# Forgetting attention: a head's keys and queries in three transfers of 128 rows, head 0's ahead of a store and the mask

## The chip, the cores and the metric

The kernel runs on one core of a Trainium2 chip, as one launch. The metric is the device time of that core in microseconds, the median over the runs of a kernel. The core has a matmul engine (TensorE, PE in the profile, with its weight loads shown apart as PEld), a vector engine (VectorE, DVE), an engine for activations and copies (ScalarE, ACT), a general one (GpSimd, POOL) and a sync engine (SyncE, SP), which here only issues transfers. Each engine takes its own instructions in order; semaphores tie them together. Transfers between the chip's memory (DRAM) and the core's on-chip memory (SBUF, 128 partitions) are carried out by 16 DMA engines. They are issued from queues: SPq is SP's, ACTq and POOLq are those of ACT and POOL.

## The reference, cut to what matters

One layer of a streaming encoder on 1024 frames of width 1024: a norm, one input projection shared by three token mixers (a gated recurrence, forgetting attention and cross-attention to 256 memory tokens), gates, an output projection, and then a gated convolutional feed-forward part. The change concerns the forgetting attention: 8 heads of width 64 over blocks of 128 queries.

```python
def _fox_mixer(q, k, v, f_logit, f_bias, q_g, k_g):
    ...
    log_f = jax.nn.log_sigmoid(f_logit.astype(jnp.float32) + f_bias.astype(jnp.float32))
    Fc = jnp.cumsum(log_f, axis=1).transpose(0, 2, 1)
    scale = FOX_DH ** -0.5
    outs = []
    for blk in range(T // Q_BLOCK):
        lo, hi = blk * Q_BLOCK, (blk + 1) * Q_BLOCK
        s = (jnp.einsum('bhqd,bhkd->bhqk', qh[:, :, lo:hi], kh[:, :, :hi]) * scale
             + Fc[:, :, lo:hi, None] - Fc[:, :, None, :hi])
        mask = (lo + jnp.arange(Q_BLOCK))[:, None] >= jnp.arange(hi)[None, :]
        p = jax.nn.softmax(jnp.where(mask, s, -jnp.inf), axis=-1)
        outs.append(jnp.einsum('bhqk,bhkd->bhqd', p, vh[:, :, :hi]))
```

## The kernel before, in words

Every float32 matmul is done on a high and a low part of its operands (`split`: ACT casts to the shorter format, DVE subtracts to get the rest), as three products `high*high + high*low + low*high` (`mm3`, lines 122 to 124). Large projections go by a scheme with seven block products instead of eight. The kernel goes through the input projections, the forgetting attention, the recurrence, the merge, the output projection and the feed-forward part.

**Where the keys and queries lie.** `put_fqk` (line 647) norms and turns the keys and queries of a pair `p` of heads and stores them in the DRAM tensor `kqd[p]` of shape 2 x 128 x 2 x 1024 (line 655; the last of these stores is issued at 319.44 us, just before the change's place). Index 0 of the first dimension is the keys, 1 the queries; the 128 rows are two heads of 64; then comes high or low part; then 1024 frames. A row of one part is 4 KB.

**Loads of a head.** `fox_load(h)` (line 1012) fills three tiles of 128 partitions x 1024: `kh` holds the keys' high part in both halves, `qa` the queries' high part above their low part, `kl` the keys' low part in both halves. So one matmul of `qa` with `kh` (line 1046) gives high*high + low*high, and one with `kl` (line 1047) adds the rest. Each tile is filled by two transfers of 64 rows (lines 1016 and 1017). Then come two broadcasts of the cumulated forget logits, `nf` (1020), and the values, `vhl` (1022). `kh`, `qa` and `kl` exist twice, for even and odd heads. A head's loads are queued on SPq behind the previous head's first store of results (`yd<-yp`, line 1093); the tile `yp` has a single buffer.

**Attention of a head.** `fox_attn(h)` (line 1027) goes through the 8 query blocks in pairs: POOL adds the mask `mskf` to a block of `nf` (1040), PE makes the logits (1046, 1047), DVE adds the bias and takes the maximum (1052), ACT takes the exponential (1062), POOL scales by the sum's reciprocal (1064), PE turns the result and multiplies by the values (1075 to 1088), ACT and DVE bring it out (1091, 1092).

**What runs beside it.** The input projections of the recurrence and the gates (`cm_unit`, line 808) come in units. A unit loads four weight blocks `ur` (818), adds some of them up on POOL (`us`, 758), casts them on ACT and DVE (`uh`, `ul`, 752 and 753), and has seven products; the results pass through the tile `uo`, of which there are two (803, 804, 796, 797), to a store on SPq (`put_hg`, line 805) or POOL's queue (798), or for gates on ACT's. The first six of the seven steps of unit 0 are laid out ahead of the attention (line 998). They hold the store of the recurrence's queries of head 0, second half of the frames (line 805), which the change moves.

**What sets the order.** Python code lays out all instructions; a planner then orders those of each engine and queue before the run, by priority and by a timeline that it works out with costs of its own. `weave` mixes attention steps with projection steps; `ahead(..., AHEAD)` and `tc.high_priority(n)` give instructions the priority of a place `n` instructions earlier (`AHEAD` is 300); `tc.issue_after(x)` queues what stands in its block behind `x`, if on the same engine, without a wait for `x` to finish. The mask `mskf` is loaded with a priority of 600 instructions ahead (line 1010), `resets` (1007) with none.

Of the kernel before, what the change touches and what calls it, by code (L numbers as in the profile page):

```python
# [9 lines left out]
F32 = mybir.dt.float32  # L10
# [5 lines left out]
P = 128  # L16
T = 1024
# [16 lines left out]
AHEAD = 300  # L34
# [35 lines left out]
def tile_block(ctx: ExitStack, tc: tile.TileContext, xT, x_rows, memT, vec, fbias, mats, hmask, w_ff, w_tm, w_cm,  # L70
               w_mkv, w_br, w_out, w_up, w_dn, outT):
    nc = tc.nc
    V, S, G, PE, SP = nc.vector, nc.scalar, nc.gpsimd, nc.tensor, nc.sync
# [69 lines left out]
    def combine(dst, ps, e, c):  # L143

        if e is None:
            S.activation(dst, ps, AF.Copy, scale=-1.0 if c else 1.0)
        elif c:
            V.scalar_tensor_tensor(out=dst, in0=ps, scalar=-1.0, in1=e, op0=ALU.mult, op1=ALU.subtract)
        else:
            V.tensor_add(dst, ps, e)  # L150
# [6 lines left out]
    kqd = [tc.dram_tile([2, P, 2, T], F32, name=f"kqd{p}") for p in range(4)]  # L157
# [615 lines left out]
    def out_tile():  # L773
        return ur.tile([P, HB], F32, tag="uo", name="uo", bufs=2)

    def put_gate(i):
# [7 lines left out]
            S.dma_start(gd[i, n], t)  # L784
        return put

    def put_hg(what, h):
        def put(c, n, ps, e):
            t = out_tile()
            dst = hgd[h][what][:, n * HB:(n + 1) * HB]  # L790
            if what == 0:
                if e is None:
                    S.activation(t, ps, AF.Tanh, scale=-0.5)
                else:
                    combine(t, ps, e, c)
                    S.activation(t, t, AF.Tanh, scale=0.5)
                G.tensor_scalar(t, t, TMIN, TMAX, ALU.max, ALU.min)
                G.dma_start(dst, t)
                return
            else:  # L800
                z = e if e is not None else ur.tile([P, HB], F32, tag="ue", name="ue", bufs=3)
                combine(z, ps, e, c)
                S.activation(t, z, AF.Tanh, scale=0.5)
                V.scalar_tensor_tensor(out=t, in0=t, scalar=1.0, in1=z, op0=ALU.add, op1=ALU.mult)
            SP.dma_start(dst, t)
        return put

    def cm_unit(u, puts):
# [43 lines left out]
    def puts_of(what, i):  # L852
        return put_gate(i) if what == "gt" else put_hg("fqg".index(what), i)
# [152 lines left out]
    resets = pf.tile([P, 256], F32, tag="resets", name="resets")  # L1006
    SP.dma_start(resets, mats[:, 3 * P:3 * P + 256])
    mskf = pf.tile([P, P], F32, tag="mskf", name="mskf")
    with tc.high_priority(2 * AHEAD):
        SP.dma_start(mskf, mats[:, 2 * P:3 * P])  # L1010

    def fox_load(h):
        p, a = h // 2, slice(64 * (h % 2), 64 * (h % 2) + 64)
        kh, qa, kl = (pf.tile([P, T], F32R, tag=f"{t}{h % 2}", name=f"{t}_{h}") for t in ("kh", "qa", "kl"))
        for t, (u, v) in ((kh, (0, 0)), (qa, (2, 3)), (kl, (1, 1))):
            SP.dma_start(t[0:64, :].bitcast(F32), kqd[p][u // 2][a, u % 2, :])
            SP.dma_start(t[64:128, :].bitcast(F32), kqd[p][v // 2][a, v % 2, :])
        nf = [pf.tile([P, HB], F32, tag="nf", name="nf", bufs=3) for _ in range(2)]
        for n, t in enumerate(nf):
            SP.dma_start(t, negFd[h:h + 1, n * HB:(n + 1) * HB].partition_broadcast(P))  # L1020
        vhl = pf.tile([P, 8, P], F32R, tag="vhl", name="vhl", bufs=2)
        SP.dma_start(vhl.bitcast(F32), vhd[h // 4][:, :, h % 4, :])
        return kh, kl, qa, vhl, nf
# [3 lines left out]
    def fox_attn(h):  # L1027
        p, a = h // 2, slice(64 * (h % 2), 64 * (h % 2) + 64)
        with tc.issue_after(marks["head"].ins) if h else nullcontext():
            kh, kl, qa, vhl, nf = fox_load(h)  # L1030
# [725 lines left out]
    for a, b, own, first, c, n, sign, last, xq in (  # L1756
# [6 lines left out]
        dst = banks if own else ybanks  # L1763
# [130 lines left out]
```

## Time and profile before

| | |
|---|---|
| median of 3 runs | 1677.19 us (1676.16 to 1678.06) |
| profiled execution, its own time | 1679.46 us |
| its span, first to last instruction | 1677.7 us |
| mean granted clock of PE | 0.998 |
| busy: PE, DVE, ACT, POOL | 1654.1, 1215.9, 845.5, 441.4 us |
| `kh`, `qa`, `kl`: loads, size, median from issue to landing | 16 each, 256 KB; 4.0, 5.0, 6.4 us |
| first and last issue of a `kh` load | 322.3 and 617.2 us |

The profile is that of one execution; a row of a timeline gives start and duration in us, engine, line, operation, output and input tiles, shape and count, and in brackets how long the engine stood idle before and what released it. Rows with SPq, ACTq or POOLq are issues of transfers: their duration is that of the issue, not of the transfer. The view of the transfers counts packets (contiguous pieces moved, and tiny ones that close a transfer) and gives for each group the time from issue to landing.

### The profile page before, as it was taken

The page shows a single profiled execution, that of the slowest core. Times are in us where ns is not written, and L with a number is a line of the kernel's source. Part 1 is how long each engine was busy: PE and PEld are TensorE (multiplying, and loading weights), DVE is VectorE, ACT ScalarE, POOL GpSimd, SP SyncE. Part 2 cuts the span into 40 slices and gives each one's busy share as a digit, 9 for nine tenths or more (in the row PEclk, how much of TensorE's full clock was granted, in tenths as well). Part 3 has the DMA queues.
Part 4 walks back from the last instruction along what each step waited for, and adds up shares of the span by engine and source line. Part 5 has one row for each costly group of instructions (what it writes and reads, how often), then busy time and mean ns, then how long its engine had stood idle before and what let it go on. Part 6 is the DMA issues. An engine that isn't in the chain of part 4 may idle for free.

```text
span 1677.7 us, 24989 instructions
## 1 busy us (share of the span) xinstructions
PE 1654.1 (99%) x8915; PEld 1417.1 (84%) x8915; DVE 1215.9 (72%) x2179; ACT 845.5 (50%) x1453; POOL 441.4 (26%) x469
## 2 busy tenths in 40 slices
PE   8999999999999999999999999999999999999999
PEld 7989999777788888888888888888888888888887
DVE  7875766588786766678776868978878788675664
ACT  8655554466666565556333257544434434343332
POOL 1143543455444444223011052221111111100000
PEclk9999999999999999999999999999999999999999
DMA  7253352655455552646866899666544454394782
GB/s 283 98 189 103 130 180 107 200 191 164 157 164 154 151 157 103 200 133 217 317 183 174 253 215 224 175 190 179 146 132 126 153 149 130 133 390 150 239 283 87
DMA packets 132061, 298.20 MB, mean 178 GB/s; under 512 B 14008, under 2 KB 31672, under 8 KB 131296
## 3 DMA queue, kind: packets, MB, share of 16 engines
q1 hardware_dynamic: 100576, 210.08, 36.9%
q0 software_dynamic: 22144, 71.84, 16.8%
q10 hardware_dynamic: 9216, 14.68, 2.3%
q8 instruction: 70, 1.15, 0.3%
q14 instruction: 55, 0.45, 0.1%
HBM read 216.40 MB, written 103.22 MB: 191 GB/s over the span
## 4 chain that ended last, share of the span: by engine, by line
PE 54%; DMA 1%; DVE 0%; ACT 0%; issue 0%
PE pp L122 10%; PE pp L123 10%; PE pp L124 10%; PE lg L124 4%; PE lg L122 4%; PE lg L123 4%; PE tr L122 3%; PE tr L124 3%; PE tr L123 3%; PE po L124 1%; PE po L122 1%; PE po L123 1%; DMA yd<-hz 1%; PE lg L1194 1%; PE lg L1185 0%; PE po L1227 0%
## 5 line engine op out<-in xcount | busy, mean ns | idle before, releaser
L1374 ACT CAST wh<-s 128x512 fp32r<-128x512 f32 x84 | 51.5, 620 | 119.1 <-PE pp L123 62.5
L128 ACT CAST dwh<-wr 128x1024 fp32r<-128x1024 f32 (+1 forms) x41 | 40.2, 980 | 114.9 <-PE tr L123 39.2
L1527 POOL DMA_DIRECT2D rw<-in_w_up x40 | 21.8, 551 | 260.5 <-DVE wl L1375 165.1
L752 ACT CAST uh<-ur 128x512 fp32r<-128x512 f32 x78 | 48.2, 618 | 77.7 <-PE pp L123 67.0
L1374 ACT CAST wh<-rw 128x512 fp32r<-128x512 f32 x66 | 40.6, 622 | 77.2 <-PE pp L123 47.2
L1064 POOL TENSOR_SCALAR pt<-pt,st 128x128 f32<-128x128 f32 (+3 forms) x64 | 57.5, 900 | 57.8 <-DVE st L1063 37.9
L136 DVE TENSOR_TENSOR dwl<-wr,dwh 128x1024 fp32r<-128x1024 f32 (+1 forms) x41 | 46.3, 1129 | 34.4 <-ACT dwh L128 34.3
L1062 ACT ACTIVATE pt<-pt,st 128x128 f32<-128x128 f32 (+3 forms) x64 | 49.8, 778 | 41.7 <-DVE st L1059 36.2
L753 DVE TENSOR_TENSOR ul<-us,uh 128x512 fp32r<-128x512 f32 x72 | 54.4, 759 | 21.5 <-ACT uh L752 21.0
L122 PE MATMUL pp<-B21h,uh 128*128 128x512 f32 x168 | 66.6, 398 | 1.2 <-DVE ue L150 1.2
L753 DVE TENSOR_TENSOR ul<-ur,uh 128x512 fp32r<-128x512 f32 x78 | 62.3, 800 | 6.0 <-ACT uh L752 5.1
L124 PE MATMUL pp<-B21h,ul 128*128 128x512 f32 x168 | 66.2, 394 | 0.1
L123 PE MATMUL pp<-T2l,uh 128*128 128x512 f32 x168 | 66.3, 395 | 0.0
L758 POOL TENSOR_TENSOR us<-ur 128x512 f32<-128x512 f32 x36 | 50.9, 1413 | 58.2 <-DMA ur<-in_w_cm 44.4
L122 PE MATMUL pp<-T2h,uh 128*128 128x512 f32 x168 | 66.1, 396 | 0.0
L123 PE MATMUL pp<-B21l,uh 128*128 128x512 f32 x168 | 65.9, 392 | 0.0
L124 PE MATMUL pp<-T2h,ul 128*128 128x512 f32 x168 | 65.8, 392 | 0.0
L752 ACT CAST uh<-us 128x512 fp32r<-128x512 f32 x72 | 43.9, 615 | 37.0 <-POOL us L758 21.1
L136 DVE TENSOR_TENSOR wl<-raw,wh 128x1024 fp32r<-128x1024 f32 x29 | 40.0, 1386 | 27.5 <-ACT wh L128 27.3
L758 POOL TENSOR_TENSOR us<-us,ur 128x512 f32<-128x512 f32 x36 | 49.5, 1375 | 38.7 <-issue 33.7
L1375 DVE TENSOR_TENSOR wl<-s,wh 128x512 fp32r<-128x512 f32 x84 | 57.3, 683 | 0.9 <-ACT wh L1374 0.6
L1375 DVE TENSOR_TENSOR wl<-rw,wh 128x512 fp32r<-128x512 f32 x66 | 44.4, 686 | 15.8 <-PE pp L124 13.5
(745 smaller groups left out, 6154.5 us busy)
## 6 DMA issues: line engine op xcount, KB each, us to landing
rw<-in_w_up POOLq DMA_DIRECT2D x40, 512.0 KB, 4.8
ur<-in_w_cm SPq DMA_DIRECT2D x72, 256.0 KB, 3.7
sd<-in_w_dn POOLq DMA_DIRECT2D x30, 512.0 KB, 8.3
br<-yd SPq DMA_DIRECT2D x30, 512.0 KB, 5.1
gd<-uo ACTq DMA_DIRECT2D x48, 256.0 KB, 3.0
gt<-gd SPq DMA_DIRECT2D x48, 256.0 KB, 5.0
yd<-fc SPq DMA_DIRECT2D x44, 256.0 KB, 2.3
raw<-in_w_tm SPq DMA_DIRECT2D x20, 512.0 KB, 3.4
```

What stands on the lines that cost most here:

```text
L122: PE.matmul(ps, lh, rh, start=first, stop=False, skip_group_check=more)
L123: PE.matmul(ps, lh, rl, start=False, stop=False, skip_group_check=more)
L124: return PE.matmul(ps, ll, rh, start=False, stop=last, skip_group_check=more)
L128: S.copy(out, in_)
L136: return (sub or V).tensor_sub(l, src, h.bitcast(F32))
L752: marks["cast"] = S.copy(h, src)
L753: V.tensor_sub(l, src, h.bitcast(F32))
L758: G.tensor_add(t, a, b)
L1062: S.activation(pt[:, :ns], pt[:, :ns], AF.Exp, bias=st[:, 2:3], accum_out=st[:, 3:4])
L1064: G.tensor_scalar(pt[:, :ns], pt[:, :ns], st[:, 3:4], 0.0, ALU.mult, ALU.add)
L1374: late["cast"] = S.copy(h, src)
L1375: late["split"] = V.tensor_sub(l, src, h.bitcast(F32))
```

## The change

Three things are changed. Each of the three tiles of a head is filled by one transfer of 128 rows. For `kh` and `kl` the source is the same 64 rows named twice (a leading dimension of 2 with step 0), for `qa` the high part's 64 rows and then the low part's (the two dimensions exchanged); as the transfer is written, the tile's side has 128 rows and the source 2 x 64. For head 0 these loads are given a priority of 600 instructions ahead; the mask's load, with the same priority, is queued behind the last of them. The store of the recurrence's queries (head 0, second half) isn't issued where its data is made but kept back, and is queued behind the same load.

```diff
+    stored_late = []
+
     def put_hg(what, h):
...
-            SP.dma_start(dst, t)
+            if (what, h, n) == (1, 0, 1):
+                stored_late.append(partial(SP.dma_start, dst, t))
+            else:
+                SP.dma_start(dst, t)
...
     mskf = pf.tile([P, P], F32, tag="mskf", name="mskf")
-    with tc.high_priority(2 * AHEAD):
-        SP.dma_start(mskf, mats[:, 2 * P:3 * P])
 
     def fox_load(h):
         p, a = h // 2, slice(64 * (h % 2), 64 * (h % 2) + 64)
         kh, qa, kl = (pf.tile([P, T], F32R, tag=f"{t}{h % 2}", name=f"{t}_{h}") for t in ("kh", "qa", "kl"))
-        for t, (u, v) in ((kh, (0, 0)), (qa, (2, 3)), (kl, (1, 1))):
-            SP.dma_start(t[0:64, :].bitcast(F32), kqd[p][u // 2][a, u % 2, :])
-            SP.dma_start(t[64:128, :].bitcast(F32), kqd[p][v // 2][a, v % 2, :])
+        twice = lambda part: kqd[p][0][a, part, :].unsqueeze(0).to_broadcast([2, 64, T])
+        with nullcontext() if h else tc.high_priority(2 * AHEAD):
+            for t, src in ((kh, twice(0)), (qa, kqd[p][1][a].rearrange("a b t -> b a t")), (kl, twice(1))):
+                loaded = SP.dma_start(t.bitcast(F32), src)
+        if h == 0:
+            with tc.high_priority(2 * AHEAD), tc.issue_after(loaded.ins):
+                SP.dma_start(mskf, mats[:, 2 * P:3 * P])
+            with tc.issue_after(loaded.ins):
+                stored_late.pop()()
```

## The prediction

> **What bounds the kernel now.** I read the page first, then the waits of the matmul engine, then the timelines of the transfer queue (SPq), of ScalarE (ACT) and of the matmul engine (PE) around the loads that the change touches. The page:
>
> ```profile
> span 1677.7 us, 24989 instructions
> ...
> PE 1654.1 (99%) x8915; PEld 1417.1 (84%) x8915; DVE 1215.9 (72%) x2179; ACT 845.5 (50%) x1453; POOL 441.4 (26%) x469
> ```
>
> PE is busy for 1654.1 of 1677.7 us. All of its idle time together is 23.6 us, so no change that leaves its matmuls alone can win more, while a new wait on PE, which takes its instructions in order, is paid nearly in full. The waits of PE (total us, times, longest) that touch the attention loads:
>
> ```profile
> PE po L1087 <- DVE yp L1092: 3.4, 1, 3.4
> PE lg L1047 <- DMA kl<-kqd: 1.8, 2, 1.0
> PE lg L1046 <- DMA qa<-kqd: 1.6, 1, 1.6
> ```
>
> Only 3.4 us are waits for keys and queries (1.6 + 1.8). Where the 1.6 comes from, in order of time (start, us, engine, line):
>
> ```profile
> 319.44 0.52 SPq L655 DMA_DIRECT2D kqd<-ko  x1
> 321.42 0.33 SPq L805 DMA_DIRECT2D hgd<-uo  x1
> 321.81 0.42 SPq L1010 DMA_DIRECT2D mskf<-in_mats  x1
> 322.28 0.52 SPq L1016 DMA_DIRECT2D kh<-kqd  x1
> 325.42 0.63 ACT L803 ACTIVATE uo<-ue 128x512 f32<-128x512 f32 x1
> 325.60 0.58 SPq L1017 DMA_DIRECT2D kl<-kqd  x1
> 327.68 0.39 PE L124 MATMUL pp<-B21h,ul 128*128 128x512 f32 x1
> 329.62 0.47 PE L1046 MATMUL lg<-kh,qa 128*128 128x128 f32 x2 [1.55 <-DMA qa<-kqd]
> 333.34 0.39 PE L1047 MATMUL lg<-kl,qa 128*128 128x128 f32 x2
> ```
>
> SPq is free at 319.96 (319.44 + 0.52) but stands until 321.42 before the store of L805. The loads stand behind that store and the mask: the first starts at 322.28, the sixth at 325.60, and PE, done at 328.07, waits 1.55 us.
>
> **The change part by part.** *Order of head 0.* With loads ahead of store and mask, the first can start at 319.96 instead of 322.28, 2.3 us earlier. The store goes behind three issues of at most 0.6 us and the mask's 0.42, so to about 322.2 instead of 321.42. Its buffer, one of two `uo`, is what ACT's L803 at 325.42 writes, and the casts that PE needs are queued on ACT behind L803; nothing else on SPq between (two broadcasts, the values, `resets`) is needed sooner. At nothing if the store lands by 325.4; otherwise ACT waits as long as the loads ahead hold it up.
>
> *Three issues instead of six.* Three issues less of 0.52 to 0.58 us, some 1.7 us of SPq per head. SPq isn't what PE waits for except through those 3.4 us, so by itself this is worth at most those.
>
> *The shape.* Today each load has 64 rows as the outermost dimension on both sides. The new ones have 128 rows on the tile's side, but the source is written as 2 x 64 x 1024: outermost count 2 (a repeat for `kh` and `kl`, the high and low part for `qa`). No load of the trace has that. The nearest rows are those for another small outermost count, the store of `ffd` with 8 rows of 4 KB, against a load of 128 rows of 4 KB. Packets in the stretch 127.5 to 130.5 us, which holds only that store, then in 131 to 136 us, where what moves is the 128-row load:
>
> ```profile
> DMA packets 16, 0.03 MB, mean 11 GB/s; under 512 B 8, under 2 KB 8, under 8 KB 16
> ffd<-ff SPq DMA_DIRECT2D x1, 32.0 KB
> ```
>
> ```profile
> DMA packets 144, 0.52 MB, mean 105 GB/s; under 512 B 16, under 2 KB 16, under 8 KB 144
> q1 hardware_dynamic: 144, 0.52, 31.8%
> raw<-in_w_tm SPq DMA_DIRECT2D x1, 512.0 KB, 3.3
> ```
>
> 128 rows make 128 data packets and 16 tiny ones, one for each of the 16 engines at its end; 8 rows make 8 and only 8. So I read it that a transfer is dealt to the engines along its outermost dimension, and that 8 rows use 8 engines. The bounds for the new loads are then 16 engines, if the tile's 128 rows decide, and 2, if the source's 2 does. I take 2: the smaller count has to be cut somewhere too, and each copy of 64 rows is one piece of it.
>
> The Trainium skill, page "DMA: Bandwidth & Descriptors", section "Why a DMA increments its semaphore by 16 and not by 1", states this as a rule: the number of engines is the largest up to 16 that divides the slowest dimension of both sides. By it 2 and 128 give 2 engines, where a reading by the tile's rows alone gives 16; the 8 closing packets of the 8-row store agree, and no row here shows the case of 2.
>
> Price on two engines. Each then moves 64 packets of 4 KB per load.
>
> ```profile
> DMA  7253352655455552646866899666544454394782
> GB/s 283 98 189 103 130 180 107 200 191 164 157 164 154 151 157 103 200 133 217 317 183 174 253 215 224 175 190 179 146 132 126 153 149 130 133 390 150 239 283 87
> ...
> kh<-kqd SPq DMA_DIRECT2D x16, 256.0 KB, 4.0
> ```
>
> The fastest slice (36th) moves 390 GB/s at a share of 0.9 or more: 24.4 to 27.1 GB/s per engine, 151 to 168 ns a packet. The 128-row load took 0.318 x 16 x 5 us = 25.4 us over 128 packets, 199 ns. I take 160 ns, since with two engines at work there is little to compete with: 10.2 us a load (9.7 to 12.7), 30.7 us for the three, which stand one behind another on the same two. Today's `kh` lands 4.0 us after its issue with 4 packets per engine, so about 3.2 us come on top. `kl` is there 33.9 us after the first issue, in place of the time at which PE asks for it. That time, from the rows of heads 1, 3 and 7 (first issue, first use of `kl`), beside 322.28 and 333.34 for head 0:
>
> ```profile
> 356.92 0.48 SPq L1093 DMA_DIRECT2D yd<-yp  x1
> 357.49 0.55 SPq L1016 DMA_DIRECT2D kh<-kqd  x1
> 367.28 0.30 PE L1047 MATMUL lg<-kl,qa 128*128 128x128 f32 x1 [0.96 <-DMA kl<-kqd]
> 456.26 0.54 SPq L1016 DMA_DIRECT2D kh<-kqd  x1
> 469.21 0.28 PE L1047 MATMUL lg<-kl,qa 128*128 128x128 f32 x1
> 617.24 0.55 SPq L1016 DMA_DIRECT2D kh<-kqd  x1
> 627.88 0.28 PE L1047 MATMUL lg<-kl,qa 128*128 128x128 f32 x1
> ```
>
> The differences are 11.1, 9.8, 13.0 and 10.6 us, mean 11. If PE's order stays as it is, PE stands 33.9 - 11 = 22.9 us in each of heads 1 to 7, 160 us; in head 0 `kl` comes at 319.96 + 33.9 = 353.9 instead of 333.34, 20.5 us. Together 181 us. What other engines owe in those stretches (the `uo` store, the weights, the broadcasts) is queued behind the same loads and lands within a few us after them, as it does today relative to `kl`; I count nothing for it.
>
> A stall of that length has a second price:
>
> ```profile
> 428.31 0.39 PE L123 MATMUL pp<-T3l,uh 128*128 128x512 f32 x1
> 428.53 0.39 PE L124 MATMUL pp<-T3h,ul 128*128 128x512 f32 x1
> 432.34 0.55 PE L1087 MATMUL po<-ph,vhl 128*128 128x256 f32 x1 [3.41 <-DVE yp L1092]
> 432.69 0.63 PE L122 MATMUL pp<-B22h,uh 128*128 128x512 f32 x1
> 437.80 0.28 PE L1088 MATMUL po<-pl,vhl 128*128 128x256 f32 x1
> ```
>
> ```profile
> 406.00:448.00 42.00, 37.73 (x190) 31.78 (x189) 31.26 (x85) 26.16 (x48) 23.16 (x24) 0.92 0.55 171
> ```
>
> After the one stall of 3.41 us the matmuls run at 0.63 us instead of 0.39, and the granted clock (the third figure from the end of the last row) is 0.92 over those 42 us. The 5.5 us from 432.34 to 437.80 hold 13 matmuls, the first two shown; 0.22 us apart, as before the stall, they would take 2.9: 2.5 us lost. Eight stalls, 20 us. The page "TensorE: Matmul & The Clock Gate" of the Trainium skill, Part 1, has the full clock back after some 3.4 us of work at half speed; by it a stall would cost 1.7 us, an estimate, and the sum would be 6 us lower. This trace shows 5.5 us at the lower clock, and the sum goes by that.
>
> Sum: 181 + 20 = 201 us on the profiled execution's 1679.46 us (span 1677.7 and 1.8 around it), 1880. That execution lies 2.3 us above the median of the runs, 1677.19, so the forecast is 1878 us. With 9.7 us a load and 14 us for the clock it is 1860, with 12.7 us a load 1940: this is the forecast's own range.
>
> **The rivals.**
>
> *PE's order makes room.* The order on PE is laid out beforehand by a planner with costs of its own; today's two waits of under 1 us for `kl` show that it expects the loads about when they come. If it knows the longer loads, it puts the first logits of the next head later and lets other work go ahead. Then only what is queued behind the loads hurts: the `yp` store (a single buffer) and the weights of the projections. A head can't be shorter than 33.9 us plus the way from the first `kl` to the store behind which the next loads go, in head 0 356.92 - 333.34 = 23.6, so 57.5; today the heads are 42.1 apart ((617.24 - 322.28) / 7). That is 15.4 x 7 + 20 = 128 us at most. At least, the two engines have 30.7 us of loads and about 19 of the rest (share 0.55 of 42 us, less today's loads of some 4): 50 per head, 7.7 x 7 = 54 us. Middle 91: 1768 us. For it: the other half of the kernel's work doesn't need these loads. Against: the diff gives the planner three transfers for six, nothing that says they are longer.
>
> *The loads spread over 16 engines, and the change does what it says.* Then `qa` lands at least 2.3 us earlier and the 1.55 us go; the two waits for `kl` (1.8 us) go with the three issues saved. 3.4 us: 1674 us, at the edge of what can be told from no change. Against it, ACT's L803 would wait for the later store: 1.5 MB at 390 GB/s is 3.9 us, so it lands near 327 instead of before 325.4, and 1 us or so comes back as a wait of PE for a cast: 1675. This case holds if all 128 rows are dealt out singly; it decides the sign.
>
> *The change doesn't do what it says.* If the loads were issued no earlier (tiles not free before 322), the spread case loses its 1.55 us and gives 1675.5; the two-engine case gets 2.3 us worse.
>
> **How the numbers follow.** A measurement of this kernel can tell about 0.2%, 3.4 us, from no change. Two engines with PE's order as today 0.48; two engines with PE's order making room 0.27; spread, in any of its forms, 0.22; something between (the three loads on different pairs of engines, so that `kl` comes after some 14 us and a head costs 3) 0.03. Of the spread case 0.08 is faster by over 0.2%, 0.13 within, 0.01 slower. The range has to reach into the spread case, since that alone is more than 2 in 10: from 1672 to 1945 us, with the forecast's own range of 1860 to 1940 inside it.
>
> **What would show it.** Right: the loads' time to landing in the list of issues rises from 4 to 6 us to over 10, 20 and 30 for `kh`, `qa` and `kl`; PE's waits name `qa` and `kl` with about 20 us each time, eight times; the granted clock falls in the slices from 330 to 800 us; the matmuls' count and the time from the end of the attention on stay as they are. Wrong: landings of 4 to 6 us (spread), or long landings without long waits of PE for `kl` but heads more than 50 us apart (order makes room).

## The result, and the profile after

The changed kernel takes 1871.37 us (median of 5 runs, 1870.48 to 1873.12) where the kernel before took 1678.06 beside it (5 runs, 1676.16 to 1680.31): a ratio of 1.115, 95% interval 1.1137 to 1.1163. The profiled execution took 1870.48 us. Its page:

```profile
span 1868.7 us, 24935 instructions
...
PE 1675.1 (90%) x8915; PEld 1431.4 (77%) x8915; DVE 1210.8 (65%) x2179; ACT 846.3 (45%) x1453; POOL 439.9 (24%) x469
...
PE   9999999448559657859999999999999999999999
...
PEclk9999999779779779879999999999999999999999
...
DMA packets 131341, 298.20 MB, mean 160 GB/s; under 512 B 13288, under 2 KB 30952, under 8 KB 130576
```

The span is 191.0 us longer (1868.7 - 1677.7). PE has the same 8915 matmuls; they keep it busy 21.0 us longer (1675.1 - 1654.1), and its idle time goes from 23.6 to 193.6 us, 170.0 more. In the slices, 46.7 us each, both losses lie from the 8th to the 18th, that is in the attention, from about 327 to 841 us. The slices from there on are full, as before.

Where the idle time lies, from the waits of PE (total us, times, longest):

```profile
PE lg L1055 <- DMA qa<-kqd: 87.7, 7, 16.2
PE lg L1056 <- DMA kl<-kqd: 73.7, 8, 10.3
PE pp L122 <- ACT ue L763: 17.5, 4, 12.5
```

Lines 1055 and 1056 are the 1046 and 1047 of before: the first logits of a head. Two rows that held 3.4 us now hold 161.4. The third row belongs with them: its longest wait, 12.5 us, stands in head 6 in the place of the wait for `qa`, which is why `qa` has only 7. ACT was itself idle there for 15.96 us, by the trace until that head's `qa` landed; what ties ACT to that load is not shown. With those 12.5 us the waits at the heads come to 173.9 us (161.4 + 12.5). The heads are counted from 0. One in order of time, head 5 (start, us, engine, line; in brackets the idle time before):

```profile
658.16 0.55 SPq L1021 DMA_DIRECT2D kh<-kqd  x1
658.80 0.53 SPq L1021 DMA_DIRECT2D qa<-kqd  x1
659.38 9.35 SPq L1021 DMA_DIRECT2D kl<-kqd  x1
668.78 9.72 SPq L1029 DMA_DIRECT2D nf<-negFd  x1
683.09 0.44 PE L1055 MATMUL lg<-kh,qa 128*128 128x128 f32 x1 [12.16 <-DMA qa<-kqd]
693.50 0.48 PE L1056 MATMUL lg<-kl,qa 128*128 128x128 f32 x1 [9.97 <-DMA kl<-kqd]
693.77 0.74 PE L124 MATMUL pp<-B11h,ul 128*128 128x512 f32 x1
698.36 0.40 PE L122 MATMUL pp<-B21h,uh 128*128 128x512 f32 x1
```

`qa` is there 24.9 us after the first issue (683.09 - 658.16) and `kl` 10.4 us after `qa` (693.50 - 683.09): one load takes 10.4 us, and two of them with 4.1 us on top make the 24.9. PE stands 12.16 + 9.97 = 22.1 us, and then its matmuls of 512 columns take up to 0.74 us, until at 698.36 one takes 0.40 again (0.39 before the change). Over the eight heads `kl` comes 34.7 us after the first issue (mean; 33.7 to 35.3). These times are those of PE's matmuls: for these loads the view of the transfers of the changed kernel gives no time to landing, so the landings that the prediction named as its first sign can't be read directly.

How many engines carry such a load shows in the count of tiny closing packets. The kernel before:

```profile
DMA packets 132061, 298.20 MB, mean 178 GB/s; under 512 B 14008, under 2 KB 31672, under 8 KB 131296
```

The bytes are the same. The packets under 512 B are 14008 - 13288 = 720 fewer. Before, 48 loads closed with 16 each, 768; now 24 loads close with 2 each, 48. The difference is 720 to the packet. Stretches of the attention show it too: in the one from 662 to 692 us, which holds most of head 5's loads and some that are queued behind them, the queue that carries them keeps the 16 engines busy for 20.5% of the time, 3.3 of them.

### The profile page after: what moved, and what is told of

Its sections match the earlier page's. It is cut to its first block, busy times and chain, and to the rows that moved or that the text cites. A ratio compares the mean times of both kernels' runs of the same rounds, so it can differ in the third digit from the quotient of the medians.

```text
span 1868.7 us, 24935 instructions
## 1 busy us (share of the span) xinstructions
PE 1675.1 (90%) x8915; PEld 1431.4 (77%) x8915; DVE 1210.8 (65%) x2179; ACT 846.3 (45%) x1453; POOL 439.9 (24%) x469
## 2 busy tenths in 40 slices
DMA packets 131341, 298.20 MB, mean 160 GB/s; under 512 B 13288, under 2 KB 30952, under 8 KB 130576
## 5 line engine op out<-in xcount | busy, mean ns | idle before, releaser
L1055 PE MATMUL lg<-kh,qa 128*128 128x512 f32 (+2 forms) x96 | 36.7, 386 | 87.8 <-DMA qa<-kqd 87.7
L1056 PE MATMUL lg<-kl,qa 128*128 128x512 f32 (+2 forms) x96 | 35.5, 374 | 73.7 <-DMA kl<-kqd 73.7
L1055 PEld LDWEIGHTS lg<-kh,qa 128*128 128x128 f32 x96 | 19.7, 208 | 93.1 <-issue 90.0
L1049 POOL TENSOR_TENSOR nfm<-nf,mskf 128x128 f32<-128x128 f32 x64 | 35.0, 547 | 231.0 <-DMA nf<-negFd 136.8
L1056 PEld LDWEIGHTS lg<-kl,qa 128*128 128x128 f32 x96 | 19.7, 207 | 78.3 <-DMA kl<-kqd 76.0
L128 ACT CAST ph<-tr 128x512 fp32r<-128x512 f32 (+1 forms) x80 | 41.6, 544 | 68.8 <-PE tr L1087 36.1
L122 PE MATMUL pp<-B21h,uh 128*128 128x512 f32 x168 | 67.1, 401 | 0.0
```

Of the source, the lines that this page charges most:

```text
L122: PE.matmul(ps, lh, rh, start=first, stop=False, skip_group_check=more)
L128: S.copy(out, in_)
L1055: PE.matmul(ps[:, :w], qa[:, tsl], kh[:, s0:s0 + w], start=True, stop=False)
L1056: PE.matmul(ps[:, :w], qa[:, tsl], kl[:, s0:s0 + w], start=False, stop=True)
```

## The experiments

The kernels are given by their edits to the changed kernel, or to the kernel before where that is said. "Order" is the change in head 0 (loads, then mask, then store), "shape" the way a load is written. An edit can make the planner lay out the instructions anew; where two kernels have one order, the text says so.

**The same three loads with 64 outermost.** In the source the dimensions are exchanged; PE, DVE, ACT and POOL have the same instructions in the same order as in the changed kernel.

```diff
-        twice = lambda part: kqd[p][0][a, part, :].unsqueeze(0).to_broadcast([2, 64, T])
+        twice = lambda part: kqd[p][0][a, part, :].unsqueeze(1).to_broadcast([64, 2, T])
...
-            for t, src in ((kh, twice(0)), (qa, kqd[p][1][a].rearrange("a b t -> b a t")), (kl, twice(1))):
+            for t, src in ((kh, twice(0)), (qa, kqd[p][1][a]), (kl, twice(1))):
```

So the tile's rows hold each source row twice in succession instead of one block of 64 behind another, and `qa` holds its high and low rows in turn; the products summed in the logits are the same.

> The changed kernel with one thing altered: the source of the three loads is written 64 x 2 x 1024 instead of 2 x 64 x 1024, so that the two copies of a row (or its high and low part) lie in neighbouring partitions in all three tiles; the sum over partitions is the same. The instructions of the four compute engines stand in the same order as in the changed kernel. Theory (the outermost count of 2 leaves two engines to each load): the loads go over 16 engines, kl lands within 7 us of the first issue instead of about 35, PE's waits for qa and kl fall from 161 us to under 5, the clock stays at 1.0, 1670 to 1680 us. Rival (reading the same rows twice, or 128 rows in one transfer, is slow in itself): 1860 us or more, landings as in the changed kernel. Rival (the moved store and mask cost the time): 1860 us or more with short landings.

Measured: 1677.59 us, ratio 1.0001 (0.9992 to 1.001). Its packets, the issues with their time to landing, and the waits of PE that are now longest:

```profile
DMA packets 131677, 298.20 MB, mean 178 GB/s; under 512 B 13624, under 2 KB 31288, under 8 KB 130912
...
kh<-kqd SPq DMA_DIRECT2D x8, 512.0 KB, 4.7
qa<-kqd SPq DMA_DIRECT2D x8, 512.0 KB, 5.4
kl<-kqd SPq DMA_DIRECT2D x8, 512.0 KB, 6.3
```

```profile
PE pp L122 <- ACT ue L763: 3.2, 3, 2.4
PE tr L1084 <- DVE pl L136: 2.3, 1, 2.3
```

Closing packets: 14008 - 13624 = 384 = 24 x 16, so 24 loads fewer and all with 16. With nothing but the order of two dimensions changed, 193.8 us are gone: the shape carries the whole loss. But the 3.4 us of waits for `qa` and `kl`, which are gone here, are no gain in the time either. In the one profile of each kernel PE's idle time is 21.5 us (1675.5 - 1654.0) against 23.6, with waits for ACT and DVE where those for the loads stood, and the medians are level.

**The order alone:** six loads of 64 rows as before, with head 0's order of the changed kernel.

```diff
-            for t, src in ((kh, twice(0)), (qa, kqd[p][1][a].rearrange("a b t -> b a t")), (kl, twice(1))):
-                loaded = SP.dma_start(t.bitcast(F32), src)
+            for t, (u, v) in ((kh, (0, 0)), (qa, (2, 3)), (kl, (1, 1))):
+                SP.dma_start(t[0:64, :].bitcast(F32), kqd[p][u // 2][a, u % 2, :])
+                loaded = SP.dma_start(t[64:128, :].bitcast(F32), kqd[p][v // 2][a, v % 2, :])
```

> The other half of the change alone: six transfers of 64 rows as before, but head 0's ahead of the mask and of the late store. Theory (the order is a side matter, worth the 1.55 us wait for qa less some wait of ScalarE for the store's buffer): 1673 to 1680 us, ratio 0.998 to 1.002. Rival (holding the store back blocks ScalarE, and that carries the loss in head 0 at least): 1690 us or more, with a wait of ScalarE for the store of over 10 us.

Measured: 1685.28 us, ratio 1.0055 (1.0042 to 1.0067). ACT at the store's buffer, and PE's largest group of waits:

```profile
332.20 0.63 ACT L805 ACTIVATE uo<-ue 128x512 f32<-128x512 f32 x1 [6.76 <-DMA hgd<-uo]
```

```profile
PE lg L1056 <- DMA kl<-kqd: 5.8, 5, 1.8
```

No theory had this: the time lies between the two that were named. A wait of ACT for the moved store is there, and it made a new theory: the store comes too late behind six loads.

**That order with the store elsewhere:** the same, with the store issued at once on ACT's queue instead of behind loads and mask on SP's.

```diff
-                stored_late.append(partial(SP.dma_start, dst, t))
+                S.dma_start(dst, t)
...
-            with tc.issue_after(loaded.ins):
-                stored_late.pop()()
```

> The run with six transfers of 64 rows and head 0's new order, but with head 6's late store issued at once on ACT's queue instead of behind the loads and the mask on SP's. In the same order with the store on SP the time was 1685.28 us, and ACT waited 6.76 us for the store's buffer. If the store's lateness is what that order costs, 1676 to 1680 us and no ACT wait over 3 us for the buffer. If another order of the products costs it, whatever the store does, 1683 us or more.

"Head 6" there is a slip: the store is the one that the change moves, of the recurrence's head 0.

Measured: 1683.51 us, ratio 1.0045 (1.003 to 1.0061), some 2 us less than with the store on SP, with intervals that overlap. ACT's wait is shorter, 2.01 us at 327.05 and 2.98 at 331.65.

The store's lateness isn't most of the loss. PE's order differs from that of the kernel before in both kernels and differs between the two, and no single wait of either accounts for 6 us. The profiles say where part of it lies: PE's busy time, with the same matmuls, is 3.7 us longer than before with the store on SP (1657.8 against 1654.1) and 3.9 with it on ACT's queue (1658.0), and in both the granted clock from 365 to 380 us is 0.89, where the kernel before has 1.00. With the store on SP PE is also idle 3.4 us longer (27.0 against 23.6). What in these orders brings that about stays open.

**The shape with the old order, and the other shape with the old order.** Both are edits to the kernel before: three loads per head, head 0's loads, store and mask as they were. One writes the source with 2 outermost, the other with 64; PE, DVE, ACT and POOL have the same instructions in the same order in the two. First with 2:

```diff
-        for t, (u, v) in ((kh, (0, 0)), (qa, (2, 3)), (kl, (1, 1))):
-            SP.dma_start(t[0:64, :].bitcast(F32), kqd[p][u // 2][a, u % 2, :])
-            SP.dma_start(t[64:128, :].bitcast(F32), kqd[p][v // 2][a, v % 2, :])
+        twice = lambda part: kqd[p][0][a, part, :].unsqueeze(0).to_broadcast([2, 64, T])
+        for t, src in ((kh, twice(0)), (qa, kqd[p][1][a].rearrange("a b t -> b a t")), (kl, twice(1))):
+            SP.dma_start(t.bitcast(F32), src)
```

> The kernel before with three transfers of 128 rows per head whose source counts 2 outermost, and with head 0's loads, store and mask left in the old order. Theory: the shape alone carries the loss, so 1865 to 1885 us, with PE's waits for qa and kl at 165 to 195 us in all. Rival: the move in head 0 adds to it or saves by more than 10 us, so that this run lies outside that.

Measured: 1872.34 us, ratio 1.1158 (1.114 to 1.1175).

```profile
PE lg L1046 <- DMA qa<-kqd: 90.4, 7, 18.7
PE lg L1047 <- DMA kl<-kqd: 68.7, 8, 10.3
PE pp L122 <- ACT ue L763: 14.3, 3, 12.5
```

The time is as the theory had it. The waits that name `qa` and `kl` are 159.1 us (90.4 + 68.7), below its 165; with the 12.5 us for ACT, which stand in the place of a wait for `qa` as in the changed kernel, they are 171.6.

Then with 64, the lines added to the kernel before being:

```diff
+        twice = lambda part: kqd[p][0][a, part, :].unsqueeze(1).to_broadcast([64, 2, T])
+        for t, src in ((kh, twice(0)), (qa, kqd[p][1][a]), (kl, twice(1))):
+            SP.dma_start(t.bitcast(F32), src)
```

> The kernel before with only the shape altered: three transfers of 128 rows, source 64 x 2 x 1024, and head 0's order left as before (store and mask ahead of the loads). Theory (the held-back store makes ScalarE wait about 3 us in e1 and takes back what the loads gain; without it the wait is away): 1672 to 1677 us, ratio 0.997 to 0.9995, ScalarE's wait at the first write of uo under 1 us. Rival (the gain of three transfers is lost somewhere else, for instance in a new order of the engines): 1677 to 1683 us.

Measured: 1678.9 us, ratio 1.0006 (0.9996 to 1.0016). PE's largest group of waits, and ACT at the writes of `uo` behind the store:

```profile
PE lg L1046 <- DVE st L1052: 4.6, 5, 2.2
```

```profile
325.56 0.63 ACT L803 ACTIVATE uo<-ue 128x512 f32<-128x512 f32 x1
334.23 0.62 ACT L803 ACTIVATE uo<-ue 128x512 f32<-128x512 f32 x1
```

ACT does not wait there at all, as the theory had it, and yet the kernel is no faster: the time lies in the rival's range. So ACT's wait for the store's buffer isn't what takes the 3.4 us.

So there are two clean pairs, one in each order: 1871.37 against 1677.59, and 1872.34 against 1678.9. The shape is worth 193.8 and 193.4 us; the order, with three loads of either shape, nothing that can be told (1.0 and 1.3 us). And three issues for six gain nothing in the old order either.

**The store on ACT's queue with 64 outermost**, to see the same from the other side. It is the kernel of the first experiment (three loads with 64 outermost, the changed kernel's order) with the same edit to the store as above:

```diff
-                stored_late.append(partial(SP.dma_start, dst, t))
+                S.dma_start(dst, t)
```

> As e1 (16 engines, loads and mask as in the changed kernel), but the store that was held back is issued at once from ScalarE's own queue. Theory: head 0's loads are as early as in e1, ScalarE waits about 1 us for its data instead of 3 us for its buffer: 1671 to 1677 us. Rival (a new order decides within a few us, not this wait): 1677 to 1683 us.

Measured: 1677.24 us, ratio 0.9998 (0.9989 to 1.0007). No kernel of this study is faster than the kernel before by more than a measurement can tell. The time lies on the border between theory and rival, and ACT's wait did not go: it is 3.11 us at 327.43.

**One head alone:** the kernel before, with the changed kernel's shape in head 4 only.

```diff
+        if h == 4:
+            twice = lambda part: kqd[p][0][a, part, :].unsqueeze(0).to_broadcast([2, 64, T])
+            for t, src in ((kh, twice(0)), (qa, kqd[p][1][a].rearrange("a b t -> b a t")), (kl, twice(1))):
+                SP.dma_start(t.bitcast(F32), src)
+        else:
...
```

> The kernel before with the 2 x 64 x 1024 shape for head 4 alone, all else as before. Theory (each head pays for itself, 194 us / 8): 24 us for the wait and the clock, 1697 to 1707 us. Rival (the heads push each other, and one alone is hidden by the work beside it): under 1690 us.

Measured: 1701.81 us, ratio 1.0145 (1.012 to 1.017), 24.1 us over the 1677.74 of before beside it.

```profile
500.64 0.58 SPq L1018 DMA_DIRECT2D kh<-kqd  x1
501.31 0.52 SPq L1018 DMA_DIRECT2D qa<-kqd  x1
501.88 6.89 SPq L1018 DMA_DIRECT2D kl<-kqd  x1
523.83 0.45 PE L1051 MATMUL lg<-kh,qa 128*128 128x128 f32 x1 [10.20 <-DMA qa<-kqd]
534.19 0.47 PE L1052 MATMUL lg<-kl,qa 128*128 128x128 f32 x1 [9.91 <-DMA kl<-kqd]
```

PE stands 20.1 us in that one head, and eight times 24.1 is 193: the heads add up, each for itself, on average (in the changed kernel they stand 18.1 to 25.3 us).

**The outermost count alone.** If the source's outermost dimension sets the number of engines, then six loads of 64 rows, with no row named twice, must be slow too when the source is written as 2 x 32 rows, and less so as 4 x 16 and 8 x 8. All three have the same instructions in the same order on every engine as the kernel with the order alone, so they are to be read beside its 1685.28 us. The rows are taken in another order, the same in keys and queries.

```diff
+        mixed = lambda i: kqd[p][i // 2][a, i % 2, :].rearrange("(i c) t -> c i t", c=2)
...
+            for t, (u, v) in ((kh, (0, 0)), (qa, (2, 3)), (kl, (1, 1))):
+                SP.dma_start(t[0:64, :].bitcast(F32), mixed(u))
+                loaded = SP.dma_start(t[64:128, :].bitcast(F32), mixed(v))
```

With `c=2`:

> Six transfers of 64 rows as before, no row read twice within a transfer, in the changed kernel's order of head 0, but each source written as 2 x 32 x 1024 with the even rows first and then the odd ones (the same permutation in all tiles, so the sum is the same). Theory (the outermost count sets the number of engines): each transfer goes over two engines, six of 32 packets each, the same 192 packets per engine as in the changed kernel, kl lands about 35 us after the first issue, 1850 to 1890 us. Rival (the repeat of rows, or 128 rows in one transfer, is what costs): 1673 to 1685 us.

Measured: 1894.09 us, ratio 1.1298 (1.1277 to 1.1319), 13336 packets under 512 B (14008 - 48 x 14). That is 4 us above the theory's range and 209 above the rival's.

```profile
PE lg L1056 <- DMA qa<-kqd: 96.0, 6, 17.7
PE lg L1057 <- DMA kl<-kqd: 76.3, 8, 10.6
```

With `c=4`:

> The same with 4 x 16 x 1024. Theory: four engines, 96 packets each at 0.152 us is 14.6 us, kl lands about 19 to 20 us after the first issue instead of 35, so about 9 us of wait for each head and 1 to 3 us of clock: 1740 to 1775 us. Rival (two classes only, all 16 engines or a slow path): as the changed kernel, 1850 us or more, or as before, 1685 us or less.

Measured: 1775.47 us, ratio 1.059 (1.0571 to 1.061), just above what was expected, with 13432 packets under 512 B (14008 - 48 x 12).

```profile
653.58 0.57 SPq L1021 DMA_DIRECT2D kh<-kqd  x1
669.13 0.44 PE L1056 MATMUL lg<-kh,qa 128*128 128x128 f32 x1 [5.73 <-DMA qa<-kqd]
674.33 0.45 PE L1057 MATMUL lg<-kl,qa 128*128 128x128 f32 x1 [4.75 <-DMA kl<-kqd]
```

With `c=8`:

> As e3 and e4 with 8 x 8 x 1024. Theory: eight engines, 48 packets each at 0.152 us is 7.3 us, kl lands 10 to 13 us after the first issue, about when PE asks for it: 1683 to 1705 us (e2, the same with 16 engines, is at 1685). Rival (any outermost count under 16 is slow in the same way): 1775 us or more.

Measured: 1728.35 us, ratio 1.0303 (1.0274 to 1.0333), 13624 packets under 512 B (14008 - 48 x 8).

```profile
621.76 0.64 SPq L1021 DMA_DIRECT2D kh<-kqd  x1
633.97 0.30 PE L1056 MATMUL lg<-kh,qa 128*128 128x128 f32 x1 [2.38 <-DMA qa<-kqd]
638.34 0.45 PE L1057 MATMUL lg<-kl,qa 128*128 128x128 f32 x1 [4.08 <-DMA kl<-kqd]
```

| outermost count of the source | `kl` after the first issue, mean | time |
|---|---|---|
| 2 (128 rows, changed kernel) | 34.7 us | 1871.37 us |
| 2 (64 rows) | 35.9 us | 1894.09 us |
| 4 | 21.2 us | 1775.47 us |
| 8 | 16.1 us | 1728.35 us |

The closing packets are 2, 4 and 8 per load in each case, and the arrival and the time follow them; from 1685.28 us, with 16, nothing differs but that count. That rows named twice are read slowly is refuted by the second row, which names none twice, and by the 1677.59 us of 64 outermost, which names them all twice. With 8 the expectation missed: the loads were there at 16.1 us, not by 13, and the kernel took 23 us more than expected at most.

## Why the prediction was right

The forecast, 1878 us with its own range of 1860 to 1940, was the right case, and 1871.37 lies 7 us under its number. The whole range, 1672 to 1945 us, says little: it takes in every one of the rivals. The case itself had been given 0.48. By its steps:

- *What bounds the kernel.* PE does, and a new wait on it was paid in full: 170.0 us more of idle time and 21.0 more of busy time are the 191.0 of the span.
- *Two engines.* Right: 2 closing packets per load, and the dose of 2, 4, 8 behind it. "The smaller count has to be cut somewhere too" was an argument and no proof. The experiments show the count of the source's outermost dimension decides while the tile's side has 64 or 128 rows. The rule of the Trainium skill, page "DMA: Bandwidth & Descriptors", section "Why a DMA increments its semaphore by 16 and not by 1", the largest number up to 16 that divides the slowest dimension of both sides, agrees with all of them: 2, 4, 8, and 16 for the count of 64.
- *The price of a load.* 160 ns a packet and 10.2 us a load were forecast. From `qa` to `kl` it took 10.4 us, 162 ns for each of 64 packets on an engine. On top of the loads came 4.1 us instead of 3.2. `kl` came at 34.7 us after the first issue instead of 33.9.
- *The stall.* Forecast 22.9 us in heads 1 to 7 and 20.5 in head 0, together 181, where the waits at the heads came to 173.9 and the idle time, without the 3.4 of before, grew by 170.0. It is the largest error, and lies in when PE asks: the sum counted 11 us between first issue and first use of `kl`, from the order of the kernel before, but PE's order is laid out anew, and PE spent 13.0 us there on other work (34.7 less 173.9 / 8). It stands first for `qa` (or in head 6 for ACT) and then for `kl`, where the sum had one wait for `kl`. In head 5 22.1 us were lost, in the single head 20.1.
- *The clock.* Forecast 20 us from the one stall of before, measured 21.0 (PE's busy time, with the same matmuls), 2.6 per head. That eight was the right count is a little luck: each head has two waits, but next to no matmuls stand between them (0.4 us of work in head 5, 683.09 to 693.50 less the wait of 9.97). The shorter price worked out from the page "TensorE: Matmul & The Clock Gate" of the Trainium skill, Part 1, would have been 14 us, an estimate; in head 5 the slow matmuls go on for 4.9 us (698.36 - 693.50), so here the trace of before was the better guide.
- *Nothing for what is queued behind the loads.* Right in the sum, but not free of waits. In head 0 of the changed kernel the mask and the store stand behind the third load on SPq:

```profile
319.94 9.54 SPq L1021 DMA_DIRECT2D kl<-kqd  x1
329.52 9.72 SPq L1024 DMA_DIRECT2D mskf<-in_mats  x1
339.35 0.98 SPq L1026 DMA_DIRECT2D hgd<-uo  x1
342.58 0.77 PE L1055 MATMUL lg<-kh,qa 128*128 128x128 f32 x2 [16.19 <-DMA qa<-kqd]
353.33 0.80 PE L1056 MATMUL lg<-kl,qa 128*128 128x128 f32 x2 [9.14 <-DMA kl<-kqd]
354.10 0.63 ACT L805 ACTIVATE uo<-ue 128x512 f32<-128x512 f32 x1 [29.35 <-DMA hgd<-uo]
```

  The store "to about 322.2" went out at 339.35, since two issues took nearly 10 us each where 0.6 was counted, and ACT stood 29.35 us for its buffer. PE was waiting for `qa` and `kl` over most of that time, and the kernel with the same shape and the store and mask in their old place takes 1872.34 us, so it cost nothing that can be told. That is an accident of this shape: a forecast of the store's place has to count the time of the issues ahead of it.
- *The order of head 0 and three issues for six.* The first issue came at 318.35 instead of 322.28 us. Of that the change gave 2.3 us, as forecast: in the changed kernel the issue starts with ACT's write of the store's data (318.38), in the kernel before 2.24 us after it (320.04). The rest is where that write itself fell in the two executions. So the loads are issued earlier and the change does what it says. But these two parts together gained nothing, in any shape. The spread rival's 1674 us (3.4 us less) isn't what its case gave, 1677.59; its 1675, with a wait of ACT for the store's buffer, had the wait right, 2.99 us and then 2.19 at the next write, but not that it costs. The kernel before already waits longer at that next write, for the other buffer, whose store POOL's queue carries:

```profile
333.16 0.63 ACT L803 ACTIVATE uo<-ue 128x512 f32<-128x512 f32 x1 [6.11 <-DMA hgd<-uo]
```

  And with the old order and 64 outermost ACT does not wait at all and the time is 1678.9. What takes the place of the 3.4 us is not shown.
- *The other rivals.* PE's order did not make room: heads are 67.1 us apart ((787.85 - 318.35) / 7, from the first issues of the heads 0 and 7) and PE waits in each; in its order `kl`'s matmul even stands closer behind `qa`'s than before. "Different pairs" is out: `qa` and `kl` come 10.4 us apart.

## What to carry to other kernels

In these runs a load that is one transfer in the code was spread over as many engines as its source, as written, counted outermost: 2, 4 or 8, and 16 for a count of 64. So before two transfers are merged, see what that count becomes; when rows must be repeated or interleaved, put the large dimension outside and the 2 inside. In a profile, count the closing packets before and after: they give the engines per transfer, whatever the times say. Fewer issues were worth nothing here, where PE waited only 3.4 us for what that queue brings.

## What the runs showed that was not expected

*The issue itself is held.* With two engines per load, SPq took each of the first two issues in under 1 us, but the third took 9.35 us in head 5, and what stood behind it 9.72, about the time of one load (10.4). In all eight heads:

```profile
L1021 SPq DMA_DIRECT2D kl<-kqd x8: 989/8570/9545, 319.9 to 789.1; - x8
```

(duration in ns: least, median, most; the least is head 1, where the issues behind it are held instead.) In head 5 the third issue ends 10.6 us after the first (668.73 - 658.16), in the kernel with one such head 8.1 us. It looks as if two such loads were all that may be pending, but the number of loads isn't what counts: with six of half the size on two engines it is the fourth issue that is first held, for 2.2 to 4.1 us. What does count is not shown. With 4 and 8 engines per load no issue of these loads took over 1 us.

*Eight engines were slower per packet.* With 4.1 us on top taken off, as if it were the same in all three, a tile of 128 rows took 10.2 us on 2 engines ((34.7 - 4.1) / 3), 5.7 on 4 and 4.0 on 8: 160, 178 and 250 ns for each 4 KB. In the stretch of one head (654.5 to 674 us with 4, 622.5 to 638 with 8) the queue's packets took this share of the 16 engines' time:

```profile
q1 hardware_dynamic: 1667, 2.62, 41.2%
```

```profile
q1 hardware_dynamic: 1611, 2.76, 72.7%
```

That is 49 us of an engine's time per MB with 4 (0.412 x 16 x 19.5 / 2.62) and 65 with 8 (0.727 x 16 x 15.5 / 2.76); with 2 it is 45 (0.205 x 16 x 30 / 2.20, the stretch of head 5 above). So the time that an engine takes for a packet is no constant to divide by. But the number of engines alone doesn't set it: in head 4 of the kernel before, 16 engines with loads of 64 rows take 66 us per MB (90.9% of 500 to 506 us, 1.32 MB), and in head 4 of the first experiment 16 engines with loads of 128 rows take 50 (82.3% of 495.5 to 502 us, 1.73 MB), about as little as 2 or 4 engines. What sets it stays open.
